# Two scaled blocks of the down projection's weights, in small tiles and two steps sooner

## The chip, the cores and the metric

The kernel is one program on one core of a Trainium2 chip. The metric is the device time of one execution in microseconds, lower is better. The core's engines run beside each other: PE (matrix products), DVE and POOL (elementwise), ACT (activations, copies with a scale), and SP, which here only starts transfers. Each engine takes its instructions in a fixed order and waits at the head of its queue.

## The reference

It is one decoder layer in float32 on 512 tokens of width 1024: two attention branches, their gated merge, an output projection, a LayerNorm, and then the channel sub-layer, in which the change lies:

```python
u2 = x * (1.0 + sc2) + sh2
h = _causal_depthwise_conv(u2 @ w_up, conv_w, conv_b)
h_gate, h_val = jnp.split(h, 2, axis=-1)
ffn_out = (jax.nn.silu(h_gate) * h_val) @ w_down
x = _layer_norm(DEEPNORM_ALPHA * x + (1.0 + gt2) * ffn_out, ln2_g, ln2_b)
```

`w_up` is 1024 x 5632, `w_down` 2816 x 1024. `sc2`, `sh2` and `gt2` are computed in the kernel from the conditioning vector (adaLN).

## The kernel before

Every float32 operand of a matrix product is split in a high part (a copy on ACT into the type that PE reads, `hi_of`) and a low part (DVE subtracts the high part, `lo_of`); a product is three matmuls, high x high, high x low, low x high.

**Up projection.** It runs over 44 steps n (22 tiles of gate and value columns, in turn). A step takes 128 x 1024 up weights, splits them (`split_proc`: wh on ACT, L181, wl on DVE, L91), and makes 24 matmuls of 512 columns into one PSUM bank (`up_mm`, L133 to L135). ACT and DVE take the bank out with the three taps of the convolution (L1122 on ACT, L1123 and L1124 on DVE). Six of the eight banks hold running sums of the down projection in this stage, so the steps have two banks in turn: step n can start when L1124 of step n - 2 is done. After each fourth step, from step 7 on, come 18 more matmuls (`early_products`, L1074 to L1076) for one of eleven pairs p of the down projection.

**Down projection.** It is done as a Strassen-like scheme on the 2 x 2 blocks of each pair's weights (`wdp`: B11, B12, B22, B21). For a pair p three loads pass through the same ring of tiles as the up weights: a raw tile of 128 x 1024 that POOL's queue completes by an accumulating transfer (L160), B11, and the tile of sums (`pair_proc`), in which DVE adds blocks (L945, L946), ACT and DVE split, and ACT's queue stores the pair's raw tile to `t13` (L950), where a later stage reads it. That stage needs B22 of each pair also multiplied by the second half of the gate `gt2`, from a buffer `wgt` in memory. For p > 1, `pair_proc` makes that product (L944) and stores it. For p = 0 and 1 the gate isn't there in time (`ada_sum` ends it at step 11), so two items load B22 once more later, `scale_proc` multiplies it (L960), and POOL's queue stores it (L961).

**The ring.** All loads of the stage are items in one list, in the order in which the code adds them. `weights(i)` issues, on SP's queue, the loads of items up to i + 5 and processes them up to the step that is wanted. An item of 1024 columns takes one of five raw tiles (tag `raw`, `LOADS`). A tile is free again when its last reader is done: for up weights the subtraction on DVE, for a raw tile of a pair the store to `t13`, for a scaled item the store to `wgt`. SP issues in the order of the list, and a load whose tile isn't free holds up those behind it. Items of 512 columns are small tiles of a pool that is opened after the up projection (`state["late"]`). The pool of small tiles of 128 x 512 that the kernel uses everywhere is `z`, with 58 slots.

The orders on PE, DVE, ACT and POOL are made by a scheduler from the program; only SP keeps the order written.

Of the kernel before, what the change touches and what calls it, by code (L numbers as in the profile page):

```python
# [8 lines left out]
F32 = mybir.dt.float32  # L9
# [3 lines left out]
ALU = mybir.AluOpType  # L13
# [3 lines left out]
P = 128  # L17
# [33 lines left out]
def layer_kernel(ctx: ExitStack, tc: tile.TileContext, out, xT, x, cT, crow, wa0, wa1, bcol, bgt, w1, wct, wv, bf,  # L51
# [3 lines left out]
    V, S, G, PE = nc.vector, nc.scalar, nc.gpsimd, nc.tensor  # L55
# [3 lines left out]
    wgt = [tc.dram_tile([P, 512], F32, name=f"wgt_{q}") for q in range(FP)]  # L59
# [10 lines left out]
    def nm(s):  # L70
        cnt[0] += 1
        return f"{s}_{cnt[0]}"
# [4 lines left out]
    def paced(start, after):  # L77
        d = mybir.DependencyInfo(mybir.DependencyClass.Sync, mybir.DependencyReason.DATA)
        tc.add_manual_dep(start.ins, after.ins.name, d, reason="paced")
# [49 lines left out]
    def z(dt, s, shape=(P, 512)):  # L129
        return zp.tile(list(shape), dt, name=nm(s), tag="z", bufs=NZ)  # L130
# [8 lines left out]
    state = {"load": 0, "proc": 0}  # L139
    items, depth = [], [LOADS - 1]  # L140
    def add_item(src, proc, cols=1024):
        items.append([src, proc, cols, None, None])
        return len(items) - 1

    def weights(i, ahead=AHEAD):
        while state["load"] < min(len(items), i + depth[0]):
            it = items[state["load"]]
            if it[2] == 512:
                it[3] = state["late"].tile([P, 512], F32, name=nm("rl"), tag="rl", bufs=4)
            else:  # L150
                it[3] = stg.tile([P, 1024], F32, name=nm("raw"), tag="raw", bufs=LOADS)
            c = 0
            for src in it[0] if isinstance(it[0], list) else [it[0]]:
                w = src.shape[-1]
                d = nc.sync.dma_start(it[3][:, c : c + w], src)
                c += w
                if depth[0] < LOADS and state["load"] >= depth[0]:
                    paced(d, reads[state["load"] - depth[0]])
            if len(it) > 5:
                G.dma_start(it[3], it[5], accum_op=ALU.add)  # L160
            state["load"] += 1
            while state["proc"] <= state["load"] - depth[0]:
                process()
        while state["proc"] < min(len(items), i + 1 + ahead):
            process()
        return items[i][4]

    def process():
        it = items[state["proc"]]
        if state["proc"] < EARLY:  # L170
            with tc.issue_after(state["k" if state["proc"] else "after"].ins):
                it[4] = it[1](it[3])
        else:
            it[4] = it[1](it[3])
        state["proc"] += 1
        reads.append(state["read"])
# [261 lines left out]
    def vgroup(br, q, n):  # L438
        if q == 0:
            vbk[br] = [bank() for _ in range(NB)]  # L440
        ps = vbk[br]
        h, l = weights(n)
        kj = [(k, j) for k in (2 * q, 2 * q + 1) for j in range(NB)]
        if q == 3:
            kj.sort(key=lambda t: t[1])
        for k, j in kj:
            c = slice((k % 2) * 512, (k % 2 + 1) * 512)
            tb = slice(j * P, (j + 1) * P)
            PE.matmul(ps[j], uh[k][:, tb], h[:, c], start=k == 0, stop=False)
            PE.matmul(ps[j], uh[k][:, tb], l[:, c], start=False, stop=False)  # L450
            PE.matmul(ps[j], ul[k][:, tb], h[:, c], start=False, stop=k == KT - 1)
            if k == KT - 1:
                for half in range(2):
                    v_evac(br, j, half, ps[j])
            yield 3

    def proj(n, after):
        ps = bank()
        h, l = weights(n)
        for k in range(KT):  # L460
            c = slice(k * P, (k + 1) * P)
            mm3(ps, h[:, c], l[:, c], uh[k], ul[k], k == 0, k == KT - 1)
            yield 3
        after(ps)
# [104 lines left out]
    gt = [None, None]  # L569
    ada_st = {}  # L570

    def ada_proc(n):
        def f(r):
            if 8 <= n < 24:
                mod_col(2 + (n - 8) // 8, n % 8, r)
                return
            g, q = n // 4, n % 4
            if q == 0:
                ada_st[g] = z(F32, "ac2")
                V.tensor_scalar_mul(ada_st[g], r[:, 0:512], cTs[:, 0:1])  # L580
            acc = ada_st[g]
            for e in range(2):
                k = 2 * q + e
                if k > 0:
                    a = V.scalar_tensor_tensor(acc, r[:, e * 512 : (e + 1) * 512], cTs[:, k : k + 1], acc, ALU.mult, ALU.add)
                    state["read"] = a
        return f

    def ada_split(g, n):
        weights(n, 0)  # L590
        acc = ada_st[g]
        ah, al = z(F32R, "ach"), z(F32R, "acl")
        hi_of(ah, acc)
        lo_of(al, acc, ah)
        ada_st[g] = ah, al
        yield 0
# [360 lines left out]

    def scale_proc(p):
        def f(r):
            V.tensor_tensor(r[:, 0:512], r[:, 0:512], gt[1][:, 512:1024], ALU.mult)  # L960
            G.dma_start(wgt[p], r[:, 0:512])  # L961
        return f

    wui, pi, wai = [], [], {}
# [1 line left out]
    def add_pair_items(p):  # L966
        pi.append([add_item(wdp[p][:, 0:1024], raw_proc)])
        items[-1].append(wdp[p][:, 512:1536])
        pi[p].append(add_item(wdp[p][:, 0:512], halves_proc))

    def add_pair_sums(p):
        pi[p].append(add_item(wdp[p][:, 1024:2048], pair_proc(p)))

    for n in range(2 * FT):
        wui.append(add_item(wup[n], split_proc))
        if n in GTILES:
            k = GTILES.index(n)
            wai[(10, 28)[k // 4]] = add_item(wa1[(28, 24)[k // 4] + k % 4], ada_proc((28, 24)[k // 4] + k % 4))
        if n in (17, 21):
            add_item(wdp[n // 4 - 4][:, 1024:1536], scale_proc(n // 4 - 4))  # L980
        if n >= 5 and n % 4 == 1 and n < 2 * FT - 2:
            add_pair_items((n - 5) // 4)
        if n >= 6 and n % 4 == 2:
            add_pair_sums((n - 6) // 4)
# [162 lines left out]
    r = x1  # L1147
# [203 lines left out]
```

## Time and profile before

| | us |
|---|---|
| median of three runs | 760.0 (757.77 to 762.58) |
| profiled execution | 760.22 |
| its span on the core | 758.4 |
| PE busy | 736.6 (97%) |
| DVE busy | 608.5 (80%) |
| ACT busy | 384.8 (51%) |
| POOL busy | 108.5 (14%) |

The span runs from the first to the last instruction; 1.8 us of the profiled execution lie around it. The granted clock of PE is 0.996 of full speed, so no part of the time is a throttled clock. A busy share is an average over stages; what a wait is worth is read in its stage. In the trace "idle before <- X" names what ended an engine's wait.

### The profile page before, as it was taken

To read this page: it belongs to the slowest core of one execution; us is meant where nothing else is said; L and a number is where in the kernel's file an instruction comes from. 1 tells how busy PE (TensorE), PEld (TensorE's weight loads), DVE (VectorE), ACT (ScalarE), POOL (GpSimd) and SP (SyncE) were. 2 spreads that over 40 slices of the span, in tenths; PEclk is the share of its full clock that TensorE was granted. 3 is DMA by queue.
4 is the path that set the end of the run, shared out by engine and by line. 5 is a ranking of instruction groups with operands and counts; after the bars stand their busy time and mean duration, and the time that the engine had idled before them with its cause. 6 is when DMAs were issued, how large, how long until landed. Compare 5 with 4: busy or idle time off the path is not lost.

```text
span 758.4 us, 9876 instructions
## 1 busy us (share of the span) xinstructions
PE 736.6 (97%) x3478; PEld 607.2 (80%) x3478; DVE 608.5 (80%) x1017; ACT 384.8 (51%) x678; POOL 108.5 (14%) x138
## 2 busy tenths in 40 slices
PE   8999999999999999999999999999899999999993
PEld 4878888878888888788889888877688888887883
DVE  6869799887888895864687889876886687669997
ACT  4566566685866654432055563443454355446530
POOL 1026223452010011462000000000000000000010
PEclk9999999999999999999999999999999999999998
DMA  9943446313432232542074777667774674567711
GB/s 323 406 174 116 162 168 219 114 58 119 161 112 82 86 128 78 183 144 83 1 250 111 259 227 233 198 193 208 246 234 159 193 223 144 167 189 249 225 68 56
DMA packets 43252, 128.01 MB, mean 169 GB/s; under 512 B 5665, under 2 KB 6177, under 8 KB 43202
## 3 DMA queue, kind: packets, MB, share of 16 engines
q1 hardware_dynamic: 37602, 112.09, 42.4%
q0 software_dynamic: 2576, 7.41, 5.0%
q10 hardware_dynamic: 3024, 7.88, 3.0%
q8 instruction: 27, 0.44, 0.2%
q14 instruction: 23, 0.19, 0.1%
HBM read 117.07 MB, written 10.22 MB: 168 GB/s over the span
## 4 chain that ended last, share of the span: by engine, by line
PE 66%; DVE 13%; DMA 12%; issue 6%; ACT 2%; SPq 0%; ACTq 0%; POOL 0%; DVEq 0%; POOLq 0%
PE ps L135 14%; PE ps L133 14%; PE ps L134 14%; PE ps L300 5%; DVE wl L91 3%; DMA raw<-in_wdp 3%; PE ps L551 2%; PE ps L533 2%; PE ps L892 2%; PE ps L891 2%; PE ps L893 2%; DMA raw<-in_wup 2%; DMA raw<-in_wa 1%; PE ps L1075 1%; PE ps L1076 1%
## 5 line engine op out<-in xcount | busy, mean ns | idle before, releaser
L91 DVE TENSOR_TENSOR wl<-raw,wh 128x1024 fp32r<-128x1024 f32 (+2 forms) x112 | 139.9, 1249 | 57.7 <-ACT wh L181 57.3
L181 ACT ACTIVATE wh<-raw 128x1024 fp32r<-128x1024 f32 (+1 forms) x103 | 108.4, 1053 | 138.0 <-PE ps L134 63.9
L133 PE MATMUL ps<-u2h,wh 128*128 128x512 f32 (+1 forms) x376 | 141.9, 377 | 2.6 <-DVE cv L1124 2.5
L135 PE MATMUL ps<-u2h,wl 128*128 128x512 f32 (+1 forms) x376 | 141.3, 376 | 0.0
L134 PE MATMUL ps<-u2l,wh 128*128 128x512 f32 (+1 forms) x376 | 141.2, 376 | 0.0
L133 PEld LDWEIGHTS ps<-u2h,wh 128*128 128x128 f32 x376 | 70.8, 188 | 17.5 <-issue 4.8
L135 PEld LDWEIGHTS ps<-u2h,wl 128*128 128x128 f32 x376 | 70.8, 188 | 12.9
L134 PEld LDWEIGHTS ps<-u2l,wh 128*128 128x128 f32 x376 | 70.8, 188 | 12.6
L133 PE MATMUL ps<-uh,wh 128*128 128x512 f32 x200 | 79.4, 397 | 0.0
L135 PE MATMUL ps<-uh,wl 128*128 128x512 f32 x200 | 78.3, 391 | 0.9 <-DVE wl L91 0.9
L134 PE MATMUL ps<-ul,wh 128*128 128x512 f32 x200 | 78.2, 391 | 0.0
L160 POOL DMA_DIRECT2D raw<-in_wdp x11 | 9.5, 865 | 271.8 <-DVE raw L946 96.1
L135 PEld LDWEIGHTS ps<-uh,wl 128*128 128x128 f32 x200 | 37.6, 188 | 9.5 <-DVE wl L91 1.4
L513 POOL TENSOR_TENSOR pt<-pt,om 128x127 f32<-128x127 f32 (+3 forms) x32 | 43.2, 1361 | 8.0 <-DVE om L512 8.0
L133 PEld LDWEIGHTS ps<-uh,wh 128*128 128x128 f32 x200 | 37.6, 188 | 7.3
L134 PEld LDWEIGHTS ps<-ul,wh 128*128 128x128 f32 x200 | 37.7, 188 | 7.2
L1122 ACT ACTIVATE cv<-ps,cw 128x512 f32<-128x512 f32 x44 | 33.5, 766 | 16.5 <-PE ps L135 10.4
L1123 DVE SCALAR_TENSOR_TENSOR cv<-ps,cw,cv 128x511 f32<-128x511 f32 x44 | 32.6, 744 | 5.4 <-ACT cv L1122 5.4
L1130 ACT ACTIVATE cv<-cv 128x512 f32<-128x512 f32 x22 | 13.9, 630 | 39.2 <-DVE cv L1124 39.2
L1124 DVE SCALAR_TENSOR_TENSOR cv<-ps,cw,cv 128x510 f32<-128x510 f32 x44 | 32.5, 742 | 0.2
L632 POOL TENSOR_TENSOR raw<-raw,gt 128x1024 f32<-128x1024 f32 x8 | 21.3, 2669 | 67.6 <-DMA raw<-in_wo 54.5
L512 DVE TENSOR_TENSOR_SCAN om<-om,dg 128x127 f32<-128x127 f32 (+3 forms) x32 | 29.6, 981 | 0.5 <-ACT om L507 0.4
(226 smaller groups left out, 1606.7 us busy)
## 6 DMA issues: line engine op xcount, KB each, us to landing
raw<-in_wup SPq DMA_DIRECT2D x44, 512.0 KB, 4.5
raw<-in_wa SPq DMA_DIRECT2D x32, 512.0 KB, 4.2
raw<-in_wct SPq DMA_DIRECT2D x25, 512.0 KB, 3.8
raw<-in_wdp SPq DMA_DIRECT2D x22, 512.0 KB, 5.5
wa<-in_wa SPq DMA_DIRECT2D x14, 512.0 KB, 7.9
raw<-in_wdp SPq DMA_DIRECT2D x24, 256.0 KB, 5.2
raw<-in_wdp POOLq DMA_DIRECT2D x11, 512.0 KB, 7.8
t<-raw ACTq DMA_DIRECT2D x10, 512.0 KB, 4.1
```

The costliest lines, as they stand in the source:

```text
L91: state["read"] = V.tensor_tensor(o, i, fl(hi), ALU.subtract)
L133: PE.matmul(ps, wh, ah, start=first, stop=False)
L134: PE.matmul(ps, wh, al, start=False, stop=False)
L135: return PE.matmul(ps, wl, ah, start=False, stop=last)
L181: state["hi"] = S.activation(h[:, 0:cols], r[:, 0:cols], AF.Copy)
L300: PE.matmul(grp[g], w, u, start=j == 0 and n == 0, stop=j == KT - 1 and n == (1 if g == 7 else 2))
L512: V.tensor_tensor_scan(d0, d0, dg[:, 513 - (e - s) : 512][:, ::-1], 0.0, ALU.mult, ALU.max)
L513: G.tensor_tensor(pt[b][:, s : e - 1], pt[b][:, s : e - 1], om[:, s + 1 : e], ALU.mult)
L632: G.tensor_tensor(r, r, gt[0], ALU.mult)
L1122: S.activation(t, ps, AF.Identity, bias=cw[:, n, 3:4], scale=cw[:, n, 2:3])
L1123: V.scalar_tensor_tensor(t[:, 1:], ps[:, 0:511], cw[:, n, 1:2], t[:, 1:], ALU.mult, ALU.add)
L1124: V.scalar_tensor_tensor(t[:, 2:], ps[:, 0:510], cw[:, n, 0:1], t[:, 2:], ALU.mult, ALU.add)
```

## The change

The two items that scale B22 of the pairs 0 and 1 are added behind the up weights of steps 15 and 19, not behind those of 17 and 21. They are items of 512 columns, and while the late pool isn't open such an item gets a tile of the pool `z`. The scaling works in that tile.

```diff
             if it[2] == 512:
-                it[3] = state["late"].tile([P, 512], F32, name=nm("rl"), tag="rl", bufs=4)
+                late = state.get("late")
+                it[3] = late.tile([P, 512], F32, name=nm("rl"), tag="rl", bufs=4) if late else z(F32, "rs")
...
     def scale_proc(p):
         def f(r):
-            V.tensor_tensor(r[:, 0:512], r[:, 0:512], gt[1][:, 512:1024], ALU.mult)
-            G.dma_start(wgt[p], r[:, 0:512])
+            V.tensor_tensor(r, r, gt[1][:, 512:1024], ALU.mult)
+            G.dma_start(wgt[p], r)
...
-        if n in (17, 21):
-            add_item(wdp[n // 4 - 4][:, 1024:1536], scale_proc(n // 4 - 4))
+        if n in (15, 19):
+            p = (15, 19).index(n)
+            add_item(wdp[p][:, 1024:1536], scale_proc(p), 512)
```

Lines behind the first edit are one higher in the changed kernel, those behind the last one two higher. The order of the instructions moves on four engines. On SP's queue, before, from the up weights of step 15 to those of step 20 (in_wup: up weights, in_wa: adaLN weights, in_wdp: down weights; raw_4730 is the first scaled item):

```order
L155 DMA raw_4683<-in_wup 128x1024
L155 DMA raw_4685<-in_wup 128x1024
L155 DMA raw_4687<-in_wa 128x1024
L155 DMA raw_4728<-in_wup 128x1024
L155 DMA raw_4730<-in_wdp 128x512
L155 DMA raw_4792<-in_wdp 128x1024
L155 DMA raw_4834<-in_wdp 128x512
L155 DMA raw_4836<-in_wup 128x1024
L155 DMA raw_4892<-in_wdp 128x1024
L155 DMA raw_4894<-in_wup 128x1024
L155 DMA raw_4896<-in_wup 128x1024
```

and now (rs_4685 and rs_4910 are the scaled items, raw_4794, raw_4797 and raw_4842 the loads of pair 3):

```order
L156 DMA raw_4683<-in_wup 128x1024
L156 DMA rs_4685<-in_wdp 128x512
L156 DMA raw_4687<-in_wup 128x1024
L156 DMA raw_4730<-in_wa 128x1024
L156 DMA raw_4732<-in_wup 128x1024
L156 DMA raw_4794<-in_wdp 128x1024
L156 DMA raw_4797<-in_wdp 128x512
L156 DMA raw_4840<-in_wup 128x1024
L156 DMA raw_4842<-in_wdp 128x1024
L156 DMA raw_4908<-in_wup 128x1024
L156 DMA rs_4910<-in_wdp 128x512
L156 DMA raw_4912<-in_wup 128x1024
```

The scaled item stands ahead of step 16's weights in place of ahead of pair 3, and the second one ahead of step 20's. In the ring, the load of step 19 (before raw_4894, now raw_4908) comes behind a load of sums that took the scaled item's tile before and takes the adaLN item's now.

On DVE, before, from the sums of pair 2 to the first tap of step 13 (cv_4661):

```order
L944 TENSOR_TENSOR wg_4623<-raw_4617,gt_4554 128x512
L585 SCALAR_TENSOR_TENSOR ac_852_4504<-raw_4687,cTs,ac_852_4504 128x512
L945 TENSOR_TENSOR raw_4617<-raw_4617,raw_4501 128x512
L91 TENSOR_TENSOR wl_4694<-raw_4685,wh_4693 128x1024
L946 TENSOR_TENSOR raw_4617<-raw_4617 128x512
L91 TENSOR_TENSOR wdl_4629<-raw_4617,wdh_4627 128x512
L585 SCALAR_TENSOR_TENSOR ac_852_4504<-raw_4687,cTs,ac_852_4504 128x512
L91 TENSOR_TENSOR wdl_4630<-raw_4617,wdh_4628 128x512
L928 TENSOR_TENSOR xn_3742<-xn_3742,lnr_4257 128x512
L960 TENSOR_TENSOR raw_4730<-raw_4730,gt_4554 128x512
L1123 SCALAR_TENSOR_TENSOR cv_4661<-ps_4614,cw,cv_4661 128x511
```

and now:

```order
L945 TENSOR_TENSOR wg_4623<-raw_4617,gt_4554 128x512
L929 TENSOR_TENSOR xn_3742<-xn_3742,lnr_4257 128x512
L946 TENSOR_TENSOR raw_4617<-raw_4617,raw_4501 128x512
L947 TENSOR_TENSOR raw_4617<-raw_4617 128x512
L91 TENSOR_TENSOR wdl_4629<-raw_4617,wdh_4627 128x512
L91 TENSOR_TENSOR wdl_4630<-raw_4617,wdh_4628 128x512
L1125 SCALAR_TENSOR_TENSOR cv_4661<-ps_4614,cw,cv_4661 128x511
```

The low part of step 16 (wl_4694), the two adaLN rows (L585) and the scaling (L960) are no longer ahead of step 13's taps. They come some rows later on DVE, now:

```order
L1133 TENSOR_TENSOR cv_4604<-cv_4604,cv_4661 128x512
L961 TENSOR_TENSOR rs_4685<-rs_4685,gt_4554 128x512
L1125 SCALAR_TENSOR_TENSOR cv_4725<-ps_4682,cw,cv_4725 128x511
L1126 SCALAR_TENSOR_TENSOR cv_4725<-ps_4682,cw,cv_4725 128x510
L91 TENSOR_TENSOR wl_4696<-raw_4687,wh_4695 128x1024
L586 SCALAR_TENSOR_TENSOR ac_852_4504<-raw_4730,cTs,ac_852_4504 128x512
L1057 TENSOR_TENSOR sg_897_4788<-cv_4604 128x256
L586 SCALAR_TENSOR_TENSOR ac_852_4504<-raw_4730,cTs,ac_852_4504 128x512
L1125 SCALAR_TENSOR_TENSOR cv_4782<-ps_4729,cw,cv_4782 128x511
L91 TENSOR_TENSOR wl_4737<-raw_4732,wh_4736 128x1024
```

where step 15's first tap (cv_4782) stands ahead of step 17's low part (wl_4737). Before, step 17's low part (wl_4735) stood between the taps of step 14.

## The prediction

> **What bounds the kernel now.** I read the page first (span, busy shares), then a table of busy time by stretches, then TensorE's own timeline for its gaps, then the chain of waits inside the affected stretch, and last what the load queue (SP) waits for.
>
> ```profile
> span 758.4 us, 9876 instructions
> PE 736.6 (97%) x3478; PEld 607.2 (80%) x3478; DVE 608.5 (80%) x1017; ACT 384.8 (51%) x678; POOL 108.5 (14%) x138
> ```
>
> TensorE (PE) is busy for 736.6 of 758.4 us, so whatever this change brings must come out of some 22 us of gaps. The table by stretches (length, then PE, weight loads, VectorE = DVE, ScalarE = ACT, GpSimd = POOL, each with its instructions, then clock, DMA share, GB/s) tells how many of them lie where the change acts:
>
> ```profile
> 462.20:483.10 20.90, 20.90 (x93) 17.27 (x92) 20.90 (x35) 8.91 (x14) 0.00 (x0) 1.00 0.54 168
> 483.10:515.50 32.40, 31.92 (x139) 25.62 (x138) 26.06 (x45) 13.82 (x26) 2.77 (x4) 1.00 0.66 196
> 515.50:549.60 34.10, 31.55 (x134) 24.32 (x133) 24.12 (x40) 15.17 (x25) 0.95 (x2) 1.00 0.79 247
> 573.70:669.90 96.20, 96.20 (x426) 79.61 (x426) 71.63 (x114) 43.61 (x72) 3.44 (x4) 1.00 0.58 178
> ```
>
> The last row is the up projection undisturbed: 96.20 / 426 = 0.226 us per matmul. In the two middle rows 273 matmuls took 66.5 us where 273 x 0.226 = 61.7 would do: **4.8 us are lost between 483 and 550**, and that is all the up projection loses there. (The busy column shows less, since a matmul's record overhangs its successor.) The first row shows what comes before: DVE busy for 20.90 of 20.90 us, behind, while PE still runs on work in stock. In PE's timeline the longest gaps of the stretch end like this:
>
> ```profile
> 509.98 0.47 PE L133 MATMUL ps<-u2h,wh 128*128 128x512 f32 x1 [0.41 <-DVE cv L1124]
> 520.03 0.47 PE L133 MATMUL ps<-u2h,wh 128*128 128x512 f32 x1 [0.25 <-DVE cv L1124]
> 532.83 0.47 PE L133 MATMUL ps<-u2h,wh 128*128 128x512 f32 x1 [1.64 <-DVE cv L1124]
> ```
>
> PE starts a step only when DVE has taken the bank of the step before last (L1124, the last convolution tap). The chain of waits says why DVE is late:
>
> ```profile
> 485.08 6.20 DMA wgt<-raw
> ...
> 491.77 7.90 DMA raw<-in_wup
> ...
> 500.84 1.24 DVE wl L91
> ...
> 515.36 8.31 DMA t<-raw
> ...
> 523.74 4.89 DMA raw<-in_wup
> ...
> 529.80 1.23 DVE wl L91
> 531.03 0.66 DVE cv L1123
> ...
> 531.94 0.75 DVE cv L1124
> ```
>
> Read from the top: the scaled half of B22 sits in a raw tile of the ring of five until its store (485.08 + 6.20) lands; only then does SP issue the next load, and the up weights behind it leave at 491.77 and land at 499.67; after ACT's high part come DVE's low part (wl) and, behind it in DVE's order, the taps of an older step. Around 515 the second scaled pair does it again, beside the store of T13 (t). What SP waited for between 420 and 580 us (total, times, longest) names both stores:
>
> ```profile
> SPq L155 <- DVE wl L91: 67.6, 22, 6.3
> SPq L155 <- DMA t<-raw: 11.7, 4, 7.1
> SPq L155 <- DMA wgt<-raw: 11.4, 2, 5.9
> ```
>
> **The change, part by part.** *Removed:* two tiles of the ring, and so the two waits of SP for a store of `wgt`, 11.4 us of queue time. *Unchanged:* the bytes (two loads and two stores of 256 KB), the two multiplications (L960), the number of instructions on every engine. They cost nothing more and save nothing by themselves. SP's own rows of before, with the loads of the two pairs (the first of three at 480.68 and at 507.08) and the loads of sums that waited behind their stores (491.35 and 522.97):
>
> ```profile
> 464.14 3.73 SPq L155 DMA_DIRECT2D raw<-in_wup  x2
> 480.68 3.39 SPq L155 DMA_DIRECT2D raw<-in_wdp  x3
> 491.35 0.33 SPq L155 DMA_DIRECT2D raw<-in_wdp  x1
> 507.08 6.79 SPq L155 DMA_DIRECT2D raw<-in_wdp  x3
> 522.97 0.33 SPq L155 DMA_DIRECT2D raw<-in_wdp  x1
> ```
>
> The pair's loads move three places ahead in SP's queue, to just after step 15's weights (464.14) and, by the walk below, to some 494 us; their new slots in the pool of small tiles are waited for only through the output projection's matmuls, long past, or not at all. I take 0 us for these moves; issuing one earlier costs SP one issue of 0.33 us, and SP has time there.
>
> *Moved with them* is DVE's order, which the scheduler makes. These are the rows of before around the first pair, the first product on PE after step 14, and two landing times (kind, count, size, median us; the loads of up weights from 420 to 580 us, T13's store of the first pair alone):
>
> ```profile
> 477.56 0.68 DVE L944 TENSOR_TENSOR wg<-raw,gt 128x512 f32<-128x512 f32 x1
> 484.09 0.69 DVE L960 TENSOR_TENSOR raw<-raw,gt 128x512 f32<-128x512 f32 x1 [0.37 <-DMA raw<-in_wdp]
> 484.70 0.74 DVE L1123 SCALAR_TENSOR_TENSOR cv<-ps,cw,cv 128x511 f32<-128x511 f32 x1
> 485.69 0.74 DVE L1124 SCALAR_TENSOR_TENSOR cv<-ps,cw,cv 128x510 f32<-128x510 f32 x1
> 488.95 1.22 DVE L91 TENSOR_TENSOR wl<-raw,wh 128x1024 fp32r<-128x1024 f32 x1
> 490.08 0.74 DVE L1124 SCALAR_TENSOR_TENSOR cv<-ps,cw,cv 128x510 f32<-128x510 f32 x1
> 483.10 0.39 PE L1074 MATMUL ps<-wdh,fh 128*128 128x512 f32 x1
> raw<-in_wup SPq DMA_DIRECT2D x25, 512.0 KB, 4.5
> t<-raw ACTq DMA_DIRECT2D x1, 512.0 KB, 4.1
> ```
>
> Starts of neighbours give what a place in DVE's queue costs: 1.14 us for a 1024-wide row (488.95 to 490.08), 0.61 for a 512-wide L960 (484.09 to 484.70), 0.66 for a tap, 0.33 for a 256-wide one (484.70 to 485.69 is a tap and one of these). With those I walk the new order from 477.56, where both orders still agree. Step 13's taps no longer have wl of step 16 (1.14), two rows of the adaLN sum (0.66 each, they are of a tap's kind and size) and L960 (0.61) ahead of them: 3.1 us less, so L1124 of step 13 ends near 483.4 instead of 486.4, and PE, done with step 14 at 483.1, goes on without the small gap it had there. Then L1131 and the multiplication end at 485.9, step 14's taps at 487.3, wl of step 16 at 488.4 (its weights are wanted at 492.6), the adaLN rows at 490.1. **Here stands the new wait:** step 15's first tap is ahead of wl of step 17, and PE ends step 15 near 490.6. After ACT's 0.76 the tap starts at 491.4, wl of step 17 ends at 493.3, and only then is the slot free for step 19's weights. They leave at 493.4, against 491.77 before: 1.6 us later, not earlier. But nothing is in front of them any more: the sum's load leaves near 490 (before 491.35), and with 4.5 to 7.9 us to land they arrive at 498 to 501.3. DVE asks for them at 501.5. wl of step 19 ends by 502.7 to 503.6, step 17's taps follow by 506.8 to 507.6, and PE wants that bank at 509.8 (step 18's end, 508.9, and four products). The gap of 0.41 goes. At the second pair the walk gives 518.0 for the load of step 23 (before 523.74), because it no longer queues behind the sum's load, which waited for a `wgt` store until 522.97, nor takes the slot of T13's store, which passes to the small B11 load. wl of step 23 then ends at 526.1, and step 20's taps at 527.8 where PE wants their bank at 529.4. The gap of 1.64 goes too.
>
> *Sum.* The walk leaves no gap over; bounds are 0 (the gaps only move) and 4.8 us (all go). I take **4.0 us**: the walk is nearer to the full 4.8, and its slacks (1.6 to 3 us) are of the size of what one late landing costs (7.9 against 4.5), so I leave 0.8 to one of them. Against the profiled execution's own 760.2 us that gives **756.2 us**; the median of the runs shown is 760.0, so it serves for both. The runs shown reach from 757.8 to 762.6.
>
> A rule that speaks against this: the Trainium skill, "DMA: Bandwidth & Descriptors", section "Issuing engines are not separate DMA queues", says that transfers started from SP, ACT and POOL all run on the same 16 DMA engines and interleave. By it the same bytes in the same stretch would delay the up weights as much as now, and the sum would be 0; the trace agrees in part (T13's store took 8.3 us beside two `wgt` stores), but shares of 0.66 and 0.79 leave the engines room.
>
> **The rivals.**
> *A: the wait changes its name, 760.2 us.* The new order gives the slot of T13's store to the small B11 load, and the up weights of step 18 queue behind that. The second of them took 8.31 us; the B11 load waits for it, and what is behind the B11 load waits along. For it: t<-raw costs SP as much (11.7 us) as the stores that go. Against it: by the walk the store of the first pair leaves at 480.1; with the 4.1 us that it took before it lands near 484, and the up weights behind it are not wanted by DVE before 495. If it lands 8.3 us after issue at each pair, the gaps come back through another tile and nothing is won.
> *B: DVE's new waits for PE set the pace, 765.4 us.* In the walk DVE stands at three places for a tap whose matmuls are not done: 490.1 to 491.4, 497.3 to 498.9 and 513.9 to 516.1, together 5.2 us. If DVE is the engine that bounds the stretch (it was full from 462 to 483), that comes on top: 760.2 + 5.2. Against it: from 483.1 to 549.6 DVE was busy for 50.2 of 66.5 us, so 16 us are free. It decides from the point where wl of step 19 starts after 504.4, that is when step 19's weights need more than about 10 us to land; the longest load of the chain took 7.9.
> *C: the change doesn't do what it says, about 763 us.* Were a slot of the small pool not free, SP would stand there with the up weights behind it. As long as its longest wait for a wl, 6.3 us, less the slack of 3 us found above, is 3 us lost. The order names only waits that are long past.
>
> **How the numbers follow.** Forecast 0.65 (754 to 758.5), A 0.20, B 0.10, C 0.05. The likeliest time is 756.2. The range goes down to 753.5 (all of the 4.8 us and 2 us of scatter, as the runs shown scatter by 2.4 around their median) and up to 761.5, which takes in A. Outside lie most of B and C and a little below: about 0.18. One per cent, 7.6 us, is about what a measurement of this kernel can tell from no change. Faster than 752.4 would need more than all gaps of the stretch: 0.05. Slower than 767.6 needs B and some more: 0.05. Between them 0.90.
>
> **What would show it.** Right: no SP wait for a `wgt` store, the stretch from step 15 to the products of the fourth pair shorter by some 4 us, gaps before L133 there under 0.3 us, DVE waiting for PE before a tap near 490 and 514. Wrong: a gap before L133 that ends with DVE's L1124 behind a wl whose ACT part waited for up weights (A, if SP waited for t<-raw before them; B, if SP waited for wl). The end of the program, from 670 us on, should be as it was; a difference there would be outside my reasons.

## The result and the profile after

The changed kernel takes **754.68 us** (median of 8 runs, 754.30 to 755.92); the kernel before, run beside it, takes 759.17 us (8 runs, 757.16 to 762.58). The ratio is 0.9949, with a 95% interval of 0.9932 to 0.9965: 4.5 us faster by the medians. The profiled execution took 754.3 us, its span is 752.5 us.

From the page of after, the span and the busy shares:

```profile
span 752.5 us, 9875 instructions
PE 734.0 (98%) x3478; PEld 607.6 (81%) x3478; DVE 607.1 (81%) x1017; ACT 386.0 (51%) x678; POOL 109.0 (14%) x138
```

The table by stretches of after, cut near the same events as the prediction's (to the end of step 14, the two middle stretches to just behind the end of the products that the prediction calls the fourth pair's, then undisturbed steps; columns as there):

```profile
462.20:483.10 20.90, 20.90 (x93) 17.00 (x92) 20.46 (x34) 9.11 (x17) 0.00 (x0) 1.00 0.62 200
483.10:515.50 32.40, 32.40 (x144) 26.85 (x143) 28.30 (x47) 14.92 (x25) 2.87 (x4) 1.00 0.75 218
515.50:545.00 29.50, 29.50 (x132) 24.42 (x131) 21.40 (x34) 13.91 (x23) 0.86 (x1) 1.00 0.80 252
568.60:664.80 96.20, 96.20 (x426) 79.65 (x425) 71.66 (x114) 43.12 (x72) 3.45 (x4) 1.00 0.59 179
```

PE is now busy without a break in both middle stretches. From the end of step 14 to the end of those products, counted from start to start, it takes 61.2 us (482.88 to 544.08) where it took 66.5 (483.10 to 549.59). Outside it the program is as it was: 208.4 us behind it (before 208.8).

What SP waited for between 420 and 580 us of after (total, times, longest):

```profile
SPq L156 <- DVE wl L91: 76.4, 23, 6.8
SPq L156 <- DVE wdl L91: 19.7, 9, 5.5
SPq L156 <- DMA t<-raw: 12.3, 5, 7.5
```

The row for `wgt` is gone, the one for T13's store is not smaller. Of both T13 rows, though, most is one wait that ends at 437 us, ahead of the change (7.1 us before, 7.5 after). Of the rest, all three waits before (1.3, 0.4 and 3.0 us) stood right ahead of up weights; in after all stand ahead of down weights. DVE's timeline of after has the new waits of a tap for its matmuls, where the walk put two of them:

```profile
491.38 0.75 DVE L1125 SCALAR_TENSOR_TENSOR cv<-ps,cw,cv 128x511 f32<-128x511 f32 x1 [1.04 <-ACT cv L1124]
516.08 0.75 DVE L1125 SCALAR_TENSOR_TENSOR cv<-ps,cw,cv 128x511 f32<-128x511 f32 x1 [1.86 <-ACT cv L1124]
```

One thing the prediction did not look at turns out to matter. These are DVE's additions for the sums of the pairs p = 3 and p = 4, counted from 0 as in the code (the prediction and the expectations call them the third and the fourth), of before and then of after:

```profile
513.43 0.68 DVE L945 TENSOR_TENSOR raw<-raw,raw 128x512 f32<-128x512 f32 x1
542.14 0.68 DVE L945 TENSOR_TENSOR raw<-raw,raw 128x512 f32<-128x512 f32 x1
```

```profile
502.58 0.68 DVE L946 TENSOR_TENSOR raw<-raw,raw 128x512 f32<-128x512 f32 x1
529.14 0.69 DVE L946 TENSOR_TENSOR raw<-raw,raw 128x512 f32<-128x512 f32 x1
```

They run 11 and 13 us sooner, with everything that follows them: the low parts of the sums, and the store of T13 (at 504.03 and 531.13, before at 515.36 and 544.37), which frees a raw tile.

### The profile page after: what moved, and what is told of

It is laid out like the page before. It is cut to its first block, busy times and chain, and to the rows that moved or that the text cites. A ratio compares the mean times of both kernels' runs of the same rounds, so it can differ in the third digit from the quotient of the medians.

```text
span 752.5 us, 9875 instructions
## 1 busy us (share of the span) xinstructions
PE 734.0 (98%) x3478; PEld 607.6 (81%) x3478; DVE 607.1 (81%) x1017; ACT 386.0 (51%) x678; POOL 109.0 (14%) x138
## 4 chain that ended last, share of the span: by engine, by line
PE 82%; DVE 10%; DMA 3%; issue 2%; ACT 2%; POOL 0%; SPq 0%; DVEq 0%; ACTq 0%
PE ps L135 18%; PE ps L133 18%; PE ps L134 18%; PE ps L301 5%; PE ps L1077 3%; PE ps L1078 2%; PE ps L1076 2%; PE ps L552 2%; DVE wl L91 2%; PE ps L534 2%; PE ps L893 2%; PE ps L892 2%; PE ps L894 2%; PE ps L475 1%; PE ps L476 1%
## 5 line engine op out<-in xcount | busy, mean ns | idle before, releaser
L133 PE MATMUL ps<-u2h,wh 128*128 128x512 f32 (+1 forms) x376 | 141.6, 377 | 0.0
L133 PEld LDWEIGHTS ps<-u2h,wh 128*128 128x128 f32 x376 | 70.8, 188 | 13.6 <-issue 0.8
L133 PE MATMUL ps<-uh,wh 128*128 128x512 f32 x200 | 79.4, 397 | 0.0
L133 PEld LDWEIGHTS ps<-uh,wh 128*128 128x128 f32 x200 | 37.6, 188 | 7.4
```

The source lines that it names most:

```text
L133: PE.matmul(ps, wh, ah, start=first, stop=False)
```

## The experiments

Each kernel of an experiment was timed in five rounds against the kernel before on the same chip. The median of before differs from group to group (758.4 to 759.7 us), so the ratios are what compares. "Lost on PE" in the table is from one profiled execution, whose time is given beside it: from the products of pair 0 to the end of step 42, the last step but one, the time from start to start less the number of matmuls times 0.2267 us. One execution needn't be like the median: those of 1, 5, 6 and 13 are among the slowest of their kernels, those of 7, 11 and 12 among the fastest. The additions are DVE's rows as above.

| kernel | additions at | SP waits for `wgt<-raw` | lost on PE | profiled us | median us | ratio to before (95%) |
|---|---|---|---|---|---|---|
| before | 513.4, 542.1 | 11.4 | 5.4 | 760.2 | 758.4 to 759.7 | 1 |
| after | 502.6, 529.1 | 0 | 0.4 | 754.3 | 754.7 | 0.9949 (0.9932 to 0.9965) |
| 1: small tile, old place | 510.6, 535.5 | 0 | 5.3 | 759.0 | 757.6 | 0.9986 (0.9974 to 0.9998) |
| 2: raw tile, new place | 502.2, 528.6 | 7.6 | 0.3 | 753.9 | 754.6 | 0.9944 (0.9929 to 0.9959) |
| 3: raw tile, stored from a copy | 511.4, 539.9 | 0 | 3.4 | 758.7 | 758.7 | 1.0003 (0.999 to 1.0015) |
| 5: after, B11 small too | 504.3, 530.3 | 0 | 1.4 | 759.4 | 757.3 | 0.9983 (0.9973 to 0.9994) |
| 6: before, T13 stored early | 511.7, 540.0 | 11.9 | 3.7 | 760.8 | 757.9 | 0.9986 (0.9972 to 1.0001) |
| 7: as 1, T13 stored early | 510.4, 535.5 | 0 | 1.4 | 756.1 | 758.3 | 0.9981 (0.9966 to 0.9996) |
| 8: raw, steps 14 and 18 | 512.2, 529.2 | 5.5 | 1.0 | 755.4 | 754.6 | 0.9949 (0.993 to 0.9968) |
| 9: raw, steps 18 and 22 | 513.6, 540.0 | 10.1 | 2.7 | 757.5 | 755.8 | 0.9964 (0.9948 to 0.998) |
| 10: as 1, longer reach | 503.0, 528.8 | 0 | 0.3 | 755.0 | 754.9 | 0.995 (0.9936 to 0.9964) |
| 11: after, shorter reach | 508.9, 537.0 | 0 | 0.7 | 754.6 | 755.9 | 0.9975 (0.9958 to 0.9992) |
| 12: before, longer reach | 503.5, 529.5 | 10.0 | 0.8 | 754.7 | 755.8 | 0.9969 (0.9955 to 0.9984) |
| 13: after, sums entered later | 508.9, 538.5 | 0 | 2.0 | 757.2 | 755.9 | 0.9968 (0.9953 to 0.9982) |

There is no experiment 4.

### The two halves of the change, each alone (1, 2, 3), and one step on (5)

The theory was the prediction's own, "hold": a ring tile held until the `wgt` store lands stops SP. Its rival was "place": what counts is that the scaled items stand two steps sooner.

*1, the small tile at the old place.*

```diff
-        if n in (15, 19):
-            p = (15, 19).index(n)
+        if n in (17, 21):
+            p = (17, 21).index(n)
             add_item(wdp[p][:, 1024:1536], scale_proc(p), 512)
```

> Small tiles for the two scaled halves, but at the old places (behind the up weights of steps 17 and 21). Theory 'hold' (the gain comes from ring tiles that no longer stand in SP's way until the wgt store has landed): the whole gain without the new places, about 754.7 us, ratio to before 0.994, no SP wait for a wgt store, the stretch from the end of step 14 to the end of the fourth pair's products 61 to 62 us (before 66.5, after 61.2). Rival 'place' (the gain comes from the multiplications leaving the queue of DVE ahead of step 13's and 17's taps, two steps sooner): 759.2 us, ratio 1.000, stretch 66 us. I expect 'hold' with something less than all, 755 to 756.

757.6 us, ratio 0.9986: about a quarter of the gain (0.14% of 0.51%), at most half by the interval. And yet the stretch of the prediction holds no gap: PE needs 61.2 us from 482.14 to 543.34. The loss is just behind it. From PE's timeline, two steps of up weights and the start of the next, and under it the chain of waits behind the gap:

```profile
543.34 0.39 PE L133 MATMUL ps<-u2h,wh 128*128 128x512 f32 x1
...
554.00 0.39 PE L135 MATMUL ps<-u2h,wl 128*128 128x512 f32 x1
557.81 0.47 PE L133 MATMUL ps<-u2h,wh 128*128 128x512 f32 x1 [3.43 <-DVE cv L1126]
```

```profile
536.80 0.61 DVE raw L947
537.41 0.02 issue
537.44 10.66 DMA t<-raw
548.12 0.03 SPq L156
548.15 0.03 issue
548.18 5.43 DMA raw<-in_wup
553.65 0.04 issue
553.69 1.07 ACT wh L182
```

The two steps start their 48 matmuls every 0.2267 us (10.66 / 47). The chain reads: the sum of pair 4 is added late, T13's store leaves at 537.44, takes 10.66 us beside other transfers, and the up weights that are to have its tile leave only at 548.18. That is the wait of rival A, but here the up weights themselves have the tile, not the B11 load.

*2, the new place with raw tiles of the ring.*

```diff
-        if n in (17, 21):
-            add_item(wdp[n // 4 - 4][:, 1024:1536], scale_proc(n // 4 - 4))
+        if n in (15, 19):
+            p = (15, 19).index(n)
+            add_item(wdp[p][:, 1024:1536], scale_proc(p))
```

> Raw tiles of the ring as before, but at the new places (behind steps 15 and 19). Theory 'hold': SP still waits for a wgt store (some 5 us at each of the two), the gaps of TensorE move but stay: 758 to 760 us, ratio 0.998 to 1.001. Rival 'place': 754.7 us, ratio 0.994, no gap of TensorE over 0.3 us between 483 and 545. Since the adaLN load, which is needed late, now takes the first released tile, some of the wait may be harmless: I would not be surprised by half of the gain.

754.6 us: all of the gain, with the store still in SP's way. What SP waited for in this kernel, and the second store beside the load that waited for it:

```profile
SPq L155 <- DMA t<-raw: 9.5, 4, 6.1
SPq L155 <- DMA wgt<-raw: 7.6, 2, 4.8
```

```profile
497.31 0.58 POOL L961 DMA_DIRECT2D wgt<-raw  x1 [11.72 <-DVE raw L960]
```

```profile
499.70 0.33 SPq L155 DMA_DIRECT2D raw<-in_wa  x1
500.12 0.38 SPq L155 DMA_DIRECT2D raw<-in_wup  x1
```

Two waits of together 7.6 us cost nothing here: the load that stands there is one of adaLN weights, and the up weights behind it are in time at 500.12.

*3, raw tile and old place, but the product goes to a small tile and is stored from there.*

```diff
-            V.tensor_tensor(r[:, 0:512], r[:, 0:512], gt[1][:, 512:1024], ALU.mult)
-            G.dma_start(wgt[p], r[:, 0:512])
+            g = z(F32, "wg")
+            V.tensor_tensor(g, r[:, 0:512], gt[1][:, 512:1024], ALU.mult)
+            G.dma_start(wgt[p], g)
```

> Before, with the ring tile, the old place and the same store on POOL's queue, but the product written to a small tile and stored from there: the ring tile is free when DVE has multiplied, some 6 us sooner than when the store has landed. Theory 'hold': 755 to 756 us, ratio 0.994 to 0.996, the SP row for wgt gone. Rival 'place': 759.2. A third theory, 'count' (the ring is short of a tile there, whoever holds it): 757 to 759, since the load still takes one of five.

Ratio 1.0003: nothing, though no ring tile waits for a `wgt` store. So the hold, by which the prediction explained its gain, needn't be taken away (2), and to take it away alone wins little or nothing (1, 3). "Hold" alone does not explain the gain. It isn't harmless either, as experiment 6 shows below.

*5, after with the B11 halves in small tiles too.*

```diff
-        pi[p].append(add_item(wdp[p][:, 0:512], halves_proc))
+        pi[p].append(add_item(wdp[p][:, 0:512], halves_proc, 512))
```

> After, and the B11 half of every pair (512 columns in a raw tile of 1024) loaded into a small tile too, so that it no longer takes a ring tile either, among others the one that T13's store holds. If TensorE has no wait left in the up projection, as the trace of after shows, this gives nothing: 754.0 to 755.5 us, ratio 0.993 to 0.995 to before. If the waits of SP for T13's store (12.3 us in 5 waits in after) still cost something: 752 to 753.5. If the small pool gets short, a new SP wait for a small slot and 756 or more.

757.3 us, slower than after. PE loses nothing from 459 us to the end of step 42. It loses 1.4 us around 458, and the part behind step 42 takes 91.6 us where after takes 88.2; two of its gaps there (the longest wait that after has between 664 and 700 us is 0.25):

```profile
679.17 0.50 PE L1077 MATMUL ps<-wl,hv 128*128 128x512 f32 x1 [0.77 <-DVE wl L91]
691.69 1.02 PE L1076 MATMUL ps<-wdh,fh 128*128 128x512 f32 x3 [1.01 <-ACT wdh L648]
```

There was nothing left to gain in the up projection. Why the part behind it got slower was not tried; a changed order there is the likely reason.

### Who inherits the tile of T13's store (6 to 9)

New theory, "heir": in before and in 1 the up weights of steps 23 and 27 get the tile that T13's store holds; in after and in 2 less urgent loads do.

*6 and 7: before, and experiment 1, with T13's store issued by POOL right behind the accumulating load* (the two edits are the same; `it[6]` is the pair):

```diff
             if len(it) > 5:
                 G.dma_start(it[3], it[5], accum_op=ALU.add)
+                if it[6] < FP - 1:
+                    G.dma_start(t13[it[6]], it[3])
...
-        items[-1].append(wdp[p][:, 512:1536])
+        items[-1] += [wdp[p][:, 512:1536], p]
...
-                if p < FP - 1:
-                    S.dma_start(t13[p], b)
```

> Before, with T13's store moved: issued on POOL's queue as soon as the accumulating load has landed, instead of on ACT's queue behind the sum of the pair, so that it lands some 15 us sooner and is off the ring's critical slot. The scaled pairs stay as they were. Theory 'heir' (what costs is that up weights inherit the slot of a tile whose store lands late; in before the up weights of steps 23 and 27 inherit T13's slot): the losses behind T13's store go, at most 4 us, about 755 to 756.5 us, ratio 0.995 to 0.997. Rival 'hold' (the two wgt stores cost it): nothing changes, 758.4, ratio 1.000.

> The first experiment (small tiles at the old places) with T13's store issued early on POOL's queue. Theory 'heir': its one loss of 5.3 us behind T13's store goes, 752.5 to 754.7 us, ratio 0.992 to 0.995, as good as after or a little better. If the old places themselves cost something (the order of DVE around the multiplications): 757.5, as the first experiment.

757.9 and 758.3 us, ratios 0.9986 and 0.9981: little or nothing in 6, nothing on top of experiment 1 in 7. SP's waits for the store did go down:

```profile
SPq L155 <- DMA wgt<-raw: 11.9, 2, 6.1
SPq L155 <- DMA raw<-in_wup: 5.2, 4, 1.9
SPq L155 <- DMA t<-raw: 2.8, 2, 1.6
```

(kernel 6; before 11.7 for `t<-raw`). Both miss. But neither refutes "heir". In 6 the up weights now stand behind the second `wgt` store alone, and a gap behind them stays (0.92 us, at 530.65; before 1.64). From its chain:

```profile
513.30 7.83 DMA wgt<-raw
...
521.15 5.30 DMA raw<-in_wup
```

In before the two stores land 0.7 us apart there: the load that waits for `wgt` leaves at 522.97, and T13's store lands at 523.67 (515.36 + 8.31, in the prediction's chain). Had all else stayed, taking away either one alone could have won at most 0.7 us at this place; 1, 3 and 6 each take away one.

In 7, with both stores out of the way, the loss in the table does fall, from 5.3 to 1.4 us, although the sums are as late as in 1. Both kernels then lose behind step 42 (90.7 and 89.5 us from there to the end, after 88.2), in single waits of 1.80 and 1.96 us at 672.09 and 668.82 that after doesn't have. The median of 7, 758.3 us, is still 2.2 us above its profiled execution, and that part no trace shows.

*8 and 9: raw tiles as in 2, at other steps.* `(15, 19)` becomes `(14, 18)` and `(18, 22)`.

> Raw tiles at steps 14 and 18: three steps sooner than before, one sooner than in the second experiment. The framework then gives T13's slot to the up weights of step 23 again. Theory 'heir': a loss of 2 to 4 us behind T13's store comes back near step 23, 756.5 to 758.5 us, ratio 0.9975 to 1.000. Rival 'sooner' (the earlier the multiplications and stores are done, the better): 754 to 754.7 us, ratio 0.994.

> Raw tiles at steps 18 and 22: one step later than before. T13's slot goes to a load of B11 and to one of a sum up to step 23, and to up weights only for step 27. Theory 'heir': the loss of step 23 goes, some of it stays at step 27 (as where the product was stored from a copy, 3.4 us): 755.5 to 757.5 us, ratio 0.996 to 0.999. Rival 'sooner': 759 to 761, slower than before.

8 is as fast as after with the "bad" heir; 9 is faster than before although it is later. Each contradicts one of the two theories, so neither decides alone. What the table shows for all kernels so far is another thing: where the addition of pair 4 runs near 530, PE loses 1.4 us or less; where it runs at 535 or later, it loses 2.7 to 5.4 (7, with T13's store off the path and its fastest execution profiled, is the exception).

### The reach (10 to 13)

Why does the addition come sooner? `weights` is called at step n with `min(LOADS - 1, wui[n + 2] - wui[n])`: at most four items of the list may be processed ahead. The list from step 17 on, before and after:

```
before  up 17 | scaled | raw tile of pair 3 | B11 | up 18 || sum of pair 3
after   up 17 | raw tile of pair 3 | B11 | up 18 | sum of pair 3 ||
```

Up to the mark || the items are processed at step 17. The scaled half counts as one of the four, whatever tile it has, and pushes the sum of the pair over the edge: it is emitted one step later, and DVE, which works in order, comes to it after a further step's work. That is theory "reach", and it can be changed without touching the tile or the place.

*10 (on 1) and 12 (on before): one item more at steps 16, 17, 20 and 21; the same edit.*

```diff
-    def weights(i, ahead=AHEAD):
-        while state["load"] < min(len(items), i + depth[0]):
+    def weights(i, ahead=AHEAD, more=0):
+        while state["load"] < min(len(items), i + depth[0] + more):
...
-            h, l = weights(wui[n], min(LOADS - 1, wui[min(n + 2, 2 * FT - 1)] - wui[n]))
+            h, l = weights(wui[n], min(LOADS - 1 + (n in (16, 17, 20, 21)), wui[min(n + 2, 2 * FT - 1)] - wui[n]), n in (16, 17, 20, 21))
```

> The first experiment (small tiles, old places) with the reach of loading and processing one item longer while the scaled half lies within it (steps 16, 17, 20, 21). New theory 'reach': the scaled half is one of the four items that may be processed ahead of a step; at the old place it pushes the sum of the pair one step back in the program, so DVE does it 8 to 11 us later (T13's store of the third and fourth pair at 512 and 537 us instead of 504 and 531), and what waits behind it comes late. By 'reach': T13's stores near 504 and 531, under 1 us lost on TensorE in the up projection, 754 to 755.5 us, ratio 0.993 to 0.996. By 'hold' or 'place': as the first experiment, 757.6, ratio 0.9985.

> Before, with raw tiles at the old places, and only the longer reach at steps 16, 17, 20 and 21. Theory 'reach': the sums come as early as in after although SP still waits for both wgt stores: T13's stores near 504 to 506 and 531, under 1.5 us lost on TensorE, 754.5 to 756 us, ratio 0.994 to 0.997. 'Hold' or 'place': as before, ratio 1.000.

10 has the whole gain at the old place: 754.9 us, 0.995 (experiment 1 without it: 0.9986). Where 1 had its gap, PE of 10 is busy throughout:

```profile
543.30:566.00 22.70, 22.70 (x100) 18.50 (x99) 18.93 (x31) 12.22 (x20) 0.86 (x1) 1.00 0.75 235
```

12 has more than half of the gain, by the medians, with raw tiles at the old place: 755.8 us, 0.9969. Its waits of SP, its additions, and its middle stretches by the cuts of before:

```profile
SPq L155 <- DMA t<-raw: 10.9, 5, 6.9
SPq L155 <- DMA raw<-in_wup: 10.6, 5, 5.8
SPq L155 <- DMA wgt<-raw: 10.0, 2, 5.1
```

```profile
503.45 0.68 DVE L945 TENSOR_TENSOR raw<-raw,raw 128x512 f32<-128x512 f32 x1
529.51 0.69 DVE L945 TENSOR_TENSOR raw<-raw,raw 128x512 f32<-128x512 f32 x1
```

```profile
483.10:515.50 32.40, 32.24 (x143) 26.38 (x142) 27.66 (x47) 14.27 (x24) 2.86 (x4) 1.00 0.78 237
515.50:549.60 34.10, 34.10 (x152) 28.08 (x150) 23.33 (x37) 15.67 (x25) 0.86 (x1) 1.00 0.77 239
```

SP still waits 10.0 us for the two `wgt` stores, against 11.4 in before, and PE is busy throughout the second stretch. The longer reach moves the second scaled item too, though: DVE multiplies it at 508.34, before at 514.04, and the load that waits for its store leaves at 515.27, before at 522.97. So 12 keeps the length of the hold, but not its time, and how much of its gain is the sums' own it doesn't tell. 10 has no hold, and its gain over 1 is the reach alone.

*11 and 13: after, with the sums put back.* 11 lets only three items be processed ahead at the four steps, 13 enters the two sums one step later.

```diff
-            h, l = weights(wui[n], min(LOADS - 1, wui[min(n + 2, 2 * FT - 1)] - wui[n]))
+            h, l = weights(wui[n], min(LOADS - 1 - (n in (16, 17, 20, 21)), wui[min(n + 2, 2 * FT - 1)] - wui[n]))
```

```diff
-        if n >= 6 and n % 4 == 2:
+        if n in (19, 23) or n >= 6 and n % 4 == 2 and n not in (18, 22):
             add_pair_sums((n - 6) // 4)
```

> After, unchanged in tiles and places, but at steps 16, 17, 20 and 21 only three items may be processed ahead instead of four, so that the sums of the third and fourth pair stand where before has them. Theory 'reach': T13's stores near 512 and 540, 2.5 to 5 us lost on TensorE, 757 to 759 us, ratio 0.997 to 1.000. 'Hold' (no tile held by a wgt store) and 'place' (two steps sooner): both are still given, so 754.7, ratio 0.994.

> After, unchanged in tiles, places and reach, but the sums of the third and fourth pair entered one step later in the list (behind the up weights of steps 19 and 23). DVE's order becomes that of the eleventh experiment (late sums), and T13's slots pass to the up weights of steps 23 and 27 again, as in before. No tile is held by a wgt store. If late sums cost what they do because up weights wait behind T13's store: T13's stores near 512 and 538, SP waiting over 16 us for them, 3 to 5 us lost on TensorE, 757 to 759 us, ratio 0.997 to 1.000, more than in the eleventh (0.9975, 755.9). If lateness alone decides: 756, as there. If the wgt store's hold or the sooner place decides: 754.7, ratio 0.994.

755.9 us both, 0.9975 and 0.9968. By the medians two fifths to a half of the gain goes, with the tile and the place of the change left as they are; I had expected more, and both intervals overlap that of after. Nor does 11's trace, a fast execution, show the loss: PE loses 0.7 us with an addition at 537.0. 13 was to bring back the up weights behind T13's store, but it does not part "heir" from "late": SP waits 10.5 us for that store in all, not over 16, and in both kernels one load of up weights waits for it by 3.1 us (it leaves at 545.49 in 11, at 546.66 in 13). DVE's order is alike but not the same in them either; low parts and a scaling change places. What speaks against "heir" alone is 8: there up weights wait 4.0 us for T13's store, until 519.4, and PE loses 1.0 us in all. The additions of 13:

```profile
508.87 0.69 DVE L946 TENSOR_TENSOR raw<-raw,raw 128x512 f32<-128x512 f32 x1
538.49 0.68 DVE L946 TENSOR_TENSOR raw<-raw,raw 128x512 f32<-128x512 f32 x1
```

They run 6 and 9 us later than in after, not the 11 and 13 of before. That may be why less is lost; it wasn't tried.

*What a late sum of pair 4 runs into.* One row parts the kernels, and I had not looked at it. ACT scales a row of the last LayerNorm (L1119 in before), whose load SP starts at 537.36. In before, 3, 6, 9, 11 and 13, where the addition runs at 537 or later, this row stands in ACT's order ahead of the high part of pair 4's sum and (but in 6, where POOL issues it) of the pair's T13 store, and ACT waits 3.7 to 5.5 us for its load; in all the others the row stands behind them. From ACT's timelines of before and of after, where the pair's high part starts at 530.06:

```profile
544.23 1.06 ACT L1119 ACTIVATE ln<-ln 128x1024 f32<-128x1024 f32 x1 [4.81 <-DMA ln<-in_lnrow]
```

```profile
540.25 1.06 ACT L1121 ACTIVATE ln<-ln 128x1024 f32<-128x1024 f32 x1 [3.76 <-DMA ln<-in_lnrow]
```

In before the pair's products then wait for the high and the low part, 0.9 us in all:

```profile
546.59 0.50 PE L1075 MATMUL ps<-wdl,fh 128*128 128x512 f32 x1 [0.22 <-DVE wdl L91]
```

No run moves this row by itself.

**What is shown, and what stays open.** Shown: the longer reach alone, which brings the two sums forward, is worth some 0.36% where no tile is held (10 against 1) and 0.31% where the hold stays (12 against before, 0.16 to 0.45 by the interval), of the change's 0.51%. With sooner sums the tile isn't needed (2), nor the place (10). Without them the tile alone is worth about 0.14% (1), and tile and place together 0.25 to 0.3% (11, 13). The traces show three ways in which a late sum costs: for pair 4 its high part and the T13 store fall behind the LayerNorm row on ACT, T13's store lands late and up weights wait for it (the gap of 3.43 us in 1), and in before that store and a `wgt` store land together, so that either keeps the wait. Open is how the rest divides. By the intervals 11 and 1 can't be told apart, nor can 12 and 9, nor 11, 12 and 13 from after; 9 with late additions gained 0.36% in a way I can't name. No version beat after beyond its interval.

## Why the prediction was right, and where its reason was wrong

**The sum.** Forecast 4.0 us less on the profiled execution, measured 5.9 there (760.2 to 754.3) and 4.5 by the medians; 756.2 against 754.68. The term was mis-sized in two ways. The stretch lost 5.3 us, not 4.8: counted from start to start it holds 270 matmuls, while the two rows of the table add up to 273, since a record that straddles a cut is in both. And the 0.8 us that I held back for a late landing wasn't needed, as the gaps went altogether. Of the 5.3 us some 0.9 were lost inside the products of pair 4, which waited for the late sum itself behind the LayerNorm row on ACT; the walk has no such row.

**The walk** was right nearly everywhere, since it followed the new order as it stands: step 19's weights leave at 493.57 (walk 493.4), wl of step 19 starts at 501.45 (501.5), step 17's taps end at 507.4 (506.8 to 507.6), step 23's weights leave at 518.28 (518.0), step 20's taps end at 527.6 (527.8). That is why the time came out: an order that is followed as it stands holds every move, also the one that is not named. The signs it named are there: no SP wait for a `wgt` store, no gap before L133, DVE's waits for PE.

**The reason** was wrong in the main. The part "removed: two tiles of the ring, and so the two waits of SP" put the gain on the hold. The step that failed is the inference from the chain, which shows that the store's landing came last, to the claim that taking it away is what helps. Experiments 1 and 3 take it away and keep or move the loss; 2 and 12 keep it, 12 at a sooner time, and the loss goes. For step 23 the walk itself names two obstacles, the `wgt` store and the slot of T13's store; the part on what is removed, and the sum behind it, speak of the first alone, and 6 shows that the first is enough to keep a gap there. "Moved with them is DVE's order" named the right engine and the wrong rows: I walked the multiplication and the low parts from 477 on, and did not see that the sum of the pair, 11 us sooner, was the largest move in it. That the time came out for another reason than the one given is luck, as far as the reason goes. The diff shows why only when the list is counted against the four items ahead.

**Rival A** did not happen in after (T13's store costs SP 12.3 us, before 11.7, and PE none), but it is near to what experiment 1 does: had the change been the tile alone, A would have been nearly right (0.14% won). The 11.7 us that stood for A were misread: 7.1 of them lie ahead of the change. **Rival B**: DVE's waits for PE came at all three places, 1.04, 1.06 and 1.86 us (the walk's three add up to 5.1 us, not 5.2), and stayed harmless, as argued. **Rival C** did not occur: the load into the small tile leaves right behind the up weights ahead of it. SP's timeline of after:

```profile
493.57 0.33 SPq L156 DMA_DIRECT2D raw<-in_wup  x1
493.95 0.43 SPq L156 DMA_DIRECT2D rs<-in_wdp  x1
```

**The rule of shared transfers** that I set against the change (the Trainium skill, "DMA: Bandwidth & Descriptors", section "Issuing engines are not separate DMA queues": transfers started from SP, ACT and POOL share the same 16 DMA engines): the same bytes now pass with a DMA share of 0.75 and 0.80, before 0.66 and 0.79, and PE doesn't wait. The engines had room. How long one store takes isn't told by the share: T13's took 10.66 us in experiment 1 at a share of 0.89, and 3.44 us in after (from 504.03) at 0.94.

## What to carry to other kernels

A lookahead that counts items is spent by every item in it, also by those that take no slot of the ring: count what an edit to the list pushes over the edge, and look where the pushed work lands in the order of the engine behind. A wait that a chain shows is the last one, and need not be the cause; look what else ends just before it, keep it and remove something else, and see whether the time comes back. When a change does two things, run each alone before giving either of them the credit.

## What the runs showed of the hardware that I had not expected

After the gap of 3.43 us in experiment 1, PE ran at full clock for a microsecond and then at half. The table by stretches (granted clock third from the right) of experiment 1, the gap and what follows:

```profile
554.10:557.80 3.70, 0.28 (x2) 0.02 (x1) 3.48 (x7) 1.97 (x5) 0.00 (x0) 1.00 0.60 186
557.80:558.80 1.00, 0.99 (x4) 0.84 (x5) 0.97 (x3) 1.00 (x2) 0.00 (x0) 1.00 0.89 299
558.80:562.10 3.30, 3.30 (x10) 2.51 (x9) 3.27 (x5) 2.90 (x6) 0.86 (x1) 0.52 0.41 158
562.10:566.00 3.90, 3.90 (x18) 3.23 (x17) 3.88 (x9) 2.02 (x6) 0.00 (x0) 0.97 1.03 228
```

For 3.3 us the clock is 0.52, which costs some 1.6 us more (an estimate, 3.3 x 0.48): the gap's true price was near 5.3, not 3.4. In experiment 6 a shorter gap had the same end:

```profile
669.80:672.20 2.40, 0.60 (x4) 0.18 (x3) 0.60 (x2) 1.53 (x3) 0.00 (x0) 1.00 0.37 143
672.20:673.30 1.10, 1.10 (x5) 0.93 (x6) 1.10 (x3) 0.92 (x3) 0.00 (x0) 1.00 0.00 0
673.30:676.40 3.10, 3.10 (x9) 2.35 (x9) 2.92 (x5) 0.43 (x2) 0.00 (x0) 0.50 0.00 0
```

The single wait in it was 1.80 us. In 7 one of 1.96 us, until 668.82, was followed by full clock, and so in before was the one of 1.64 us that ends at 532.83. The Trainium skill, "TensorE: Matmul & The Clock Gate", Part 1, says that the clock falls to half after an idle window of about 3.4 us. Experiment 1 agrees with it; experiment 6, with less than 2.4 us, does not. What else decides, no run here shows.
